# Activation pairs fetched one pair ahead, four products per x tile, and a last tile in two halves, in a one-core encoder layer

## The chip, the cores and the metric

The kernel runs on one core of one Trainium2 chip. The metric is device time in microseconds, from the first to the last instruction of the program, with little around them; lower is better. TensorE's clock has two levels here, 2.4 GHz (granted clock 1.00) and 1.2 GHz (0.50).

## The reference

One layer of an encoder on 512 tokens of 2048 channels, in fp32. Two branches start from the same normalised input, Hyena (long convolutions) and grouped-query attention; gates merge them, one projection follows, then a feed-forward block:

```python
h = rms_norm(x, mix_norm_g)
proj = h @ w_in                      # x0, x1, hv (Hyena), q, k, v, gates
u_h = centred_short_conv(u_h, hy_conv_w, hy_conv_b)
x0, x1, hv = jnp.split(u_h, 3, axis=-1)
filt = implicit_filter(S, flt_w1, ..., flt_freq)
z = hv * x1
y_h = (bidir_fft_conv(z, filt) + hy_bias * z) * x0
q, k = axial_rope(rms_norm(q, ...)), axial_rope(rms_norm(k, ...))
y_a = block_gqa_attention(q, k, v)
g_h, g_a = jnp.split(sigmoid(g + b_gate), 2, axis=-1)
x = x + (g_h * (y_h @ w_br_hyena) + g_a * (y_a @ w_br_attn)) @ w_out
h2 = rms_norm(x, ffn_norm_g)
out = x + (silu(h2 @ w_ffn_gate) * (h2 @ w_ffn_up)) @ w_ffn_down
```

D_FF is 5632, that is 44 tiles of 128 channels; the 2048 channels are 16 tiles (KT), the 512 tokens one free dimension (S).

## The kernel before, in words

Every fp32 product is made of three matmuls (mm3, lines 175 to 178): high part by high part, high by low, low by high. So each weight tile and each activation is split: ACT casts it to the high part, and DVE subtracts that from the raw tile.

**Plain products.** wblk (lines 156 to 173) hands out 128x128 weight blocks. Eight of them are one tile of 128x1024, loaded on SP's queue (line 168), cast by ACT (line 169, wh), subtracted by DVE (line 170, wl). There are two raw buffers (wr) and three of each part. Only the first two tiles come in pieces of XW blocks. group runs the 16 k steps of one 128x512 output, 48 matmuls.

**Side work.** step() is called behind every mm3 and runs the next step of generators that were queued: the filter network (mlp_gen, filter_gen), the long convolutions (conv_gen), the attention heads. Constants such as Q_WAIT count in such steps where a generator starts. flush() runs what is left. So the order on each engine is that of the program text, and a generator's work is laid between the main products.

**Start.** For each k an x tile is loaded and split, then XW = 2 products (x1 and hv of channel tile 0) take it. Behind the loop come 16 squares and adds for the token sums, then groups px01 and phv1 of channel tile 1; in the middle of phv1 (RS_STEP) token_rstd forms the sums (rs1ss), the reciprocal root, and its broadcast over the partitions (rs1bcp, then the copy rbc). short_conv needs rbc: it is 4 instructions, 3 of them on DVE, for each of x1, hv, x0. filter_gen makes fd, bd, then hs, hd on DVE, which TensorE transposes (ktp).

**Seven-product stages.** Gates (g), feed-forward (f) and the two halves of the down projection (d, e) run a scheme with seven products in place of eight on halves of the tokens and of the channels. x_sums makes the seven sums V of a pair of activation tiles (ACT and DVE), x_split their two parts X (one ACT cast, line 809, and one DVE subtract, line 810). run then takes four raw weight tiles per group (a11, a21, a22, a12; line 822 on SP's queue) from 8 raw buffers: two that wblk uses, tag rb in pool wq, and one more. It starts with X of the first pair.

**Down projection.** Each half has a plain part first: 16 output tiles m, each a group over 6 activations. The result dp is multiplied into dt (line 1186) and added into the DRAM tile x2d by a DMA on POOL's queue (add_up). At every even m the activations of pair m // 2 are loaded from DRAM (act_raw, ACT's queue, line 1125), summed and split. tmp, with five buffers, holds act_raw and dt. Then run does 8 groups with the eight X.

**Between.** The output projection takes merged tiles ms: m_load (ACT's queue) and m_split for m = 3 to 15 stand ahead of its first weight tile. The Hyena and attention branch groups b come behind flush().

**End.** The last two output tiles are finished by out_finish: a multiply (line 1161), an add (line 1168), a DMA.

Of the kernel before, what the change touches and what calls it, by code (L numbers as in the profile page):

```python
# [16 lines left out]
P = 128  # L17
# [12 lines left out]
GATES_AHEAD = 3  # L30
MLP_WAIT = 22
Z_WAIT0 = 16
N_WARM = 10
XW = 2
RS_STEP = 8
K_WAIT = 20
Q_WAIT = (25, 21)
# [20 lines left out]
def weight_blocks():  # L58

    def cols(name, c0, nk, k0=0, w=P):  # L60
        return [(name, (k0 + k) * P, c0, w) for k in range(nk)]

    def gates(m):
        return cols("w_in", C_GH + m * P, KT) + cols("w_in", C_GA + m * P, KT)

    out = []
    for q in range(NQ):
        for c in (2 * q, 2 * q + 1):
            x1, hv = cols("w_in", C_X1 + c * P, KT), cols("w_in", C_HV + c * P, KT)
            out += [b for pair in zip(x1, hv) for b in pair] if c == 0 else x1 + hv  # L70
        for c in (2 * q, 2 * q + 1):
            out += cols("w_in", C_X0 + c * P, KT)
    for c0, m in ((C_KV, None), (C_Q, 0), (C_Q + 512, 1), (None, 2)):
        out += cols("w_in", c0, KT, w=512) if c0 is not None else []
        out += gates(m) if m is not None else []
    for m in range(KT):
        out += cols("w_br_hyena", m * P, HT) + cols("w_br_attn", m * P, HT)

    def quarters(name, c0, c1, k0=0):
        for half, c in ((0, c0), (0, c1), (1, c1), (1, c0)):  # L80
            out.extend((name, (k0 + k) * P, c, P) for k in range(half, KT, 2))

    for m in range(GATES_AHEAD, KT):
        quarters("w_in", C_GH + m * P, C_GA + m * P)
    for k in range(KT):
        out += [("w_out", k * P, m * P, P) for m in range(WIDE)]
    for m in range(WIDE, KT):
        out += cols("w_out", m * P, KT)
    for j in range(0, FT, 2):
        for name in ("w_ffn_gate", "w_ffn_up"):  # L90
            quarters(name, j * P, (j + 1) * P)
    for f0 in (0, NSTD + KT):
        for m in range(KT):
            out += cols("w_ffn_down", m * P, NSTD, k0=f0)
        for m in range(0, KT, 2):
            quarters("w_ffn_down", m * P, (m + 1) * P, f0 + NSTD)
    return out


def layer_kernel(tc, wpk, xT, par, flt, zemb, w4, decT, tbl, tb2, rope, qkg, out):  # L100
# [55 lines left out]
    def wblk(nb=1):  # L156
# [8 lines left out]
        i, n = st["tile"] - 1, XW if st["tile"] <= 2 else BLK  # L165
# [79 lines left out]
    def sumsq_add(acc, src, k, name):  # L245
        if k == 0:
            nc.scalar.activation(acc, src, AF.Square)
        else:
            sq = tmp(f"{name}{k}")
            nc.scalar.activation(sq, src, AF.Square)  # L250
            nc.vector.tensor_tensor(acc, acc, sq, ALU.add)
# [238 lines left out]
    xg, xrs = [], []  # L490
    queue(mlp_gen())
    queue(filter_gen(0))
    for k in range(KT):
# [7 lines left out]
        xrs.append(xr)  # L501
# [4 lines left out]
    acc1 = tmp("acc1")  # L506
    for k in range(KT):
        sumsq_add(acc1, xrs[k], k, "xsq")
# [35 lines left out]
    for q in range(NQ):  # L544
        zl, zf_l = [], []
        for c in range(2):
            ct = 2 * q + c
            if ct < 2:
                p1, p2 = (xps, p2nd)[ct]
            else:  # L550
                p1 = ps_tile(f"px1{ct}")
                group(p1, xg)
# [16 lines left out]
        for c in range(2):  # L569
            ct = 2 * q + c  # L570
            p0 = ps_tile(f"px0{ct}")
            group(p0, xg)
            x0st[ct] = short_conv(p0, ct, f"x0{ct}", r3.tile([P, S], F32, tag="r", bufs=16, name=f"yh{ct}"))
# [203 lines left out]
    def seven(nm, gi, nv=3):  # L777
# [82 lines left out]
        def run(groups, c_tiles, finish, rows=None, sums=None, side_pool=None, norm=None, tail=None, each=None):  # L860
# [17 lines left out]
            for n in range(groups):  # L878
# [81 lines left out]

    flush()
    ats.release()
    at.release()
    yhs = [split(r1, t, "hi", "lo", 16, 16, f"yhs{i}") for i, t in enumerate(yh)]
# [17 lines left out]
    for m in range(KT):  # L982
        gs = []
        for i, src in enumerate((yhs, yas)):
# [3 lines left out]
            bp = ps_tile(f"b{i}{m}")  # L988
            group(bp, src)
# [61 lines left out]
    for m in range(3, KT):  # L1051
        m_load(m)
        m_split(m, r1, "ms", KT - 3)
# [105 lines left out]
    def out_finish(n, i, t):  # L1159
        m = 2 * n + i  # L1160
        nc.vector.tensor_tensor(t, t, rbc2, ALU.mult)
        if n < NP - 1:
            add_up(m, t)
            if n > 0:
                nc.gpsimd.dma_start(out[m - 2], x2d[m - 2])
            return
        nc.gpsimd.dma_start(out[m - 2], x2d[m - 2])
        nc.vector.tensor_tensor(t, t, lasts[i], ALU.add)
        nc.sync.dma_start(out[m], t)
# [9 lines left out]
    for half, f0 in enumerate((0, NSTD + KT)):  # L1179
        vp = tc.alloc_tile_pool(name=f"vpd{half}", bufs=1, reuse_waits="tile")  # L1180
        x_sums, x_split, V, run = seven("de"[half], None, 2)
        for m in range(KT):
            dp = ps_tile(f"d{half}{m}")
            group(dp, [acts[j] for j in range(f0, f0 + NSTD)])
            t = tmp(f"dt{half}{m}")
            nc.vector.tensor_tensor(t, dp, rbc2, ALU.mult)
            add_up(m, t)
            if m % 2 == 0:
                j = f0 + NSTD + m
                V[m // 2] = x_sums(m // 2, act_raw(j), act_raw(j + 1))  # L1190
                x_split(m // 2, V[m // 2], (0, 7))
# [3 lines left out]
        else:  # L1195
            run(NP, c_down, out_finish, each=last_rows)
# [115 lines left out]
```

## Time and profile before

| what | us |
|---|---|
| median of three runs | 2606.41 (2604.97 to 2608.80) |
| the profiled execution | 2606.41 |
| its span | 2604.6 |
| TensorE (PE) busy in it | 2550.0, 98% |
| DVE busy | 2017.0, 77% |
| ACT busy | 1205.6, 46% |
| POOL busy | 176.4, 7% |
| mean DMA rate | 133 GB/s |

A share over the whole span says little here: the program is a row of stages, and TensorE stands still at a few of their borders only. The views to read are therefore the list of TensorE's waits, and windows around them. In a window, PEclk is the mean granted clock, DMA the busy share of the 16 DMA engines. PEld is TensorE's weight loading, which runs beside the matmuls.

### The profile page before, as it was taken

The page shows a single profiled execution, that of the slowest core. Times are in us where ns is not written, and L with a number is a line of the kernel's source. Part 1 is how long each engine was busy: PE and PEld are TensorE (multiplying, and loading weights), DVE is VectorE, ACT ScalarE, POOL GpSimd, SP SyncE. Part 2 cuts the span into 40 slices and gives each one's busy share as a digit, 9 for nine tenths or more (in the row PEclk, how much of TensorE's full clock was granted, in tenths as well). Part 3 has the DMA queues.
Part 4 walks back from the last instruction along what each step waited for, and adds up shares of the span by engine and source line. Part 5 has one row for each costly group of instructions (what it writes and reads, how often), then busy time and mean ns, then how long its engine had stood idle before and what let it go on. Part 6 is the DMA issues. An engine that isn't in the chain of part 4 may idle for free.

```text
span 2604.6 us, 35152 instructions
## 1 busy us (share of the span) xinstructions
PE 2550.0 (98%) x13426; PEld 2186.7 (84%) x13426; DVE 2017.0 (77%) x2902; ACT 1205.6 (46%) x1796; POOL 176.4 (7%) x290
## 2 busy tenths in 40 slices
PE   9999999999999999999999999999999998999899
PEld 6788888878887888888788888888888887888688
DVE  7877763657555999754799889889889878887787
ACT  6444433647343445443444444444444445444443
POOL 1000001110000000000000000000000001001111
PEclk9999999999999999999999999999999999999899
DMA  6323233222454444544223333333333357447554
GB/s 223 110 95 116 94 116 107 73 77 91 169 185 138 158 148 143 183 156 144 101 105 130 115 120 130 115 121 130 114 121 130 114 159 205 138 126 195 155 156 105
DMA packets 112821, 345.74 MB, mean 133 GB/s; under 512 B 13835, under 2 KB 15371, under 8 KB 112428
## 3 DMA queue, kind: packets, MB, share of 16 engines
q1 hardware_dynamic: 70272, 248.02, 27.2%
q0 software_dynamic: 22112, 58.73, 8.7%
q10 hardware_dynamic: 20268, 36.74, 4.6%
q8 instruction: 105, 1.72, 0.3%
q14 instruction: 64, 0.52, 0.1%
HBM read 295.21 MB, written 51.90 MB: 133 GB/s over the span
## 4 chain that ended last, share of the span: by engine, by line
PE 63%; issue 27%; DVE 4%; DMA 2%; POOL 2%; ACT 2%; SPq 0%; POOLq 0%; ACTq 0%; DVEq 0%
PE fx L118 8%; PE b L118 7%; PE px L118 7%; PE o L118 6%; PE gx L118 5%; PE fy L118 4%; PE ex L118 3%; PE q L118 3%; PE phv L118 3%; PE gy L118 3%; PE fz L118 2%; PE ey L118 2%; PE kv L118 2%; POOL x2d L1145 1%; PE g L118 1%
## 5 line engine op out<-in xcount | busy, mean ns | idle before, releaser
L170 DVE TENSOR_TENSOR wl<-wr,wh 128x1024 fp32r<-128x1024 f32 (+1 forms) x178 | 211.7, 1189 | 180.3 <-ACT wh L169 179.2
L169 ACT CAST wh<-wr 128x1024 fp32r<-128x1024 f32 (+1 forms) x178 | 182.2, 1024 | 344.5 <-PE o L118 70.3
L841 ACT CAST fwhs<-fs 128x1024 fp32r<-128x1024 f32 x176 | 184.9, 1051 | 247.7 <-PE fx L118 115.6
L841 ACT CAST fwha<-fa 128x1024 fp32r<-128x1024 f32 x132 | 138.8, 1052 | 205.8 <-PE fx L118 102.4
L842 DVE TENSOR_TENSOR fwls<-fs,fwhs 128x1024 fp32r<-128x1024 f32 x176 | 214.6, 1220 | 10.6 <-ACT fwhs L841 3.8
L118 PE MATMUL fx<-fX,fwha 128*128 128x512 f32 x704 | 178.6, 395 | 3.7 <-DVE c L937 2.1
L118 PE MATMUL fx<-fX,fwhs 128*128 128x512 f32 x704 | 177.8, 395 | 1.9 <-DVE fv L857 1.9
L118 PE MATMUL fy<-fX,fwhs 128*128 128x512 f32 x704 | 176.9, 392 | 0.0
L842 DVE TENSOR_TENSOR fwla<-fa,fwha 128x1024 fp32r<-128x1024 f32 x132 | 161.1, 1221 | 5.1 <-ACT fwha L841 1.3
L118 PE MATMUL o<-ms,wh 128*128 128x512 f32 x512 | 159.0, 392 | 1.8 <-ACT wh L169 1.8
L118 PEld LDWEIGHTS fx<-fX,fwha 128*128 128x128 f32 x704 | 127.5, 190 | 27.5 <-DVE c L937 2.3
L118 PEld LDWEIGHTS fx<-fX,fwhs 128*128 128x128 f32 x704 | 127.7, 190 | 25.2 <-DVE fv L857 2.2
L118 PEld LDWEIGHTS fy<-fX,fwhs 128*128 128x128 f32 x704 | 126.6, 189 | 22.6
L118 PE MATMUL d<-act,wh 128*128 128x512 f32 x384 | 118.1, 389 | 0.0
L118 PEld LDWEIGHTS o<-ms,wh 128*128 128x128 f32 x512 | 96.8, 189 | 22.4 <-ACT wh L169 2.2
L118 PE MATMUL px<-xh,wh 128*128 128x512 f32 x272 | 109.2, 401 | 1.4 <-ACT wh L169 1.3
L118 PE MATMUL px<-xh,wl 128*128 128x512 f32 x272 | 107.5, 395 | 3.0 <-DVE wl L170 3.0
L835 DVE TENSOR_TENSOR fs<-fa,fa 128x1024 f32<-128x1024 f32 x88 | 106.9, 1215 | 0.3 <-DMA fa<-wpk 0.2
L118 PE MATMUL px<-xl,wh 128*128 128x512 f32 x272 | 107.1, 394 | 0.0
L835 DVE TENSOR_TENSOR fs<-fs,fa 128x1024 f32<-128x1024 f32 x88 | 107.0, 1215 | 0.1
L118 PEld LDWEIGHTS fx<-fX,fwla 128*128 128x128 f32 x704 | 96.5, 191 | 7.0
L118 PEld LDWEIGHTS fy<-fX,fwls 128*128 128x128 f32 x704 | 96.2, 190 | 6.9
(1224 smaller groups left out, 6247.8 us busy)
## 6 DMA issues: line engine op xcount, KB each, us to landing
fa<-wpk SPq DMA_DIRECT2D x176, 512.0 KB, 3.5
wr<-wpk SPq DMA_DIRECT2D x170, 512.0 KB, 3.5
ga<-wpk SPq DMA_DIRECT2D x52, 512.0 KB, 3.5
da<-wpk SPq DMA_DIRECT2D x32, 512.0 KB, 3.6
ea<-wpk SPq DMA_DIRECT2D x32, 512.0 KB, 3.6
actd<-c POOLq DMA_DIRECT2D x40, 256.0 KB, 4.9
actr<-actd ACTq DMA_DIRECT2D x40, 256.0 KB, 4.5
x2d<-dt POOLq DMA_DIRECT2D x32, 256.0 KB, 5.2
```

The source lines that it names most:

```text
L118: tc.keep_in_program_order(nc.tensor.matmul(out, lhsT=lhsT, rhs=rhs, start=start, stop=stop, **kw))
L169: nc.scalar.copy(st["hi"][:, c], st["raw"][:, c])
L170: nc.vector.tensor_tensor(st["lo"][:, c], st["raw"][:, c], st["hi"][:, c].bitcast(F32), ALU.subtract)
L835: nc.vector.tensor_tensor(t, a, b, ALU.add)
L841: nc.scalar.copy(hi, w)
L842: nc.vector.tensor_tensor(lo, w, hi.bitcast(F32), ALU.subtract)
L1145: nc.gpsimd.dma_start(x2d[m], t, accum_op=ALU.add)
```

## The change

Six parts, in the program's order.

1. XW becomes 4: the x loop feeds four products (x1 and hv of channel tiles 0 and 1), with the weights packed in that order. The first weight tile comes in pieces of two blocks, the second of four. The squares go into the loop. The group that token_rstd interrupts is now px00 (x0 of channel tile 0).
2. Q_WAIT of the second attention group is 26 steps instead of 21.
3. The first two Hyena branch groups (HYENA_FIRST) and the split of their inputs stand ahead of flush().
4. m_load and m_split for m = 3 to 15 move into the k loop of the output projection, five ahead.
5. Down halves: act_raw is issued one pair ahead, dt goes into raw buffers (tag rb, two outputs in one), the last pair's X is split in two cuts.
6. The last output tile is finished in two halves of 256 columns.

```diff
-XW = 2
+XW = 4
-Q_WAIT = (25, 21)
+Q_WAIT = (25, 26)
...
-        i, n = st["tile"] - 1, XW if st["tile"] <= 2 else BLK
+        i, n = st["tile"] - 1, {1: XW // 2, 2: XW}.get(st["tile"], BLK)
...
         for i in range(XW):
             wh, wl = wblk()
             mm3(xps[i], wh, wl, hi, lo, k == 0, k == KT - 1)
             step()
-    acc1 = tmp("acc1")
-    for k in range(KT):
-        sumsq_add(acc1, xrs[k], k, "xsq")
+        sumsq_add(acc1, xr, k, "xsq", work)
...
-    p2nd = [ps_tile("px01"), ps_tile("phv1")]
-    group(p2nd[0], xg)
-    group(p2nd[1], xg, 0, RS_STEP)
+    px00 = ps_tile("px00")
+    group(px00, xg, 0, RS_STEP)
     gen = token_rstd(acc1, "rs1", rs1)
     next(gen)
-    group(p2nd[1], xg, RS_STEP, KT)
+    group(px00, xg, RS_STEP, KT)
...
+    yhs = [split(r1, t, "hi", "lo", 16, 16, f"yhs{i}") for i, t in enumerate(yh)]
+    bps = [ps_tile(f"b0{m}") for m in range(HYENA_FIRST)]
+    for bp in bps:
+        group(bp, yhs)
     flush()
...
-    for m in range(3, KT):
-        m_load(m)
-        m_split(m, r1, "ms", KT - 3)
...
     for k in range(KT):
+        for m in range(max(3, len(ms)), min(k + 5, KT)):
+            m_load(m)
+            m_split(m, r1, "ms", KT - 3)
         for op in ops:
...
+        pairs = [[act_raw(f0 + NSTD + i) for i in (0, 1)]]
         for m in range(KT):
             dp = ps_tile(f"d{half}{m}")
             group(dp, [acts[j] for j in range(f0, f0 + NSTD)])
-            t = tmp(f"dt{half}{m}")
+            if m % 2 == 0:
+                t2 = wq.tile([P, 2 * S], F32, tag="rb", bufs=NRAW - 3, name=f"dt{half}{m}")
+            t = t2[:, m % 2 * S:(m % 2 + 1) * S]
             nc.vector.tensor_tensor(t, dp, rbc2, ALU.mult)
             add_up(m, t)
             if m % 2 == 0:
-                j = f0 + NSTD + m
-                V[m // 2] = x_sums(m // 2, act_raw(j), act_raw(j + 1))
-                x_split(m // 2, V[m // 2], (0, 7))
+                p = m // 2
+                if p + 1 < NP:
+                    pairs.append([act_raw(f0 + NSTD + m + i) for i in (2, 3)])
+                V[p] = x_sums(p, *pairs[p])
+                x_split(p, V[p], (0, 7) if p + 1 < NP else (0, 3, 7))
...
                 finish(n, 0, c0)
+                if halves and n == groups - 1:
+                    finish(n, 1, c1, slice(H, S))
                 d = ev(f"d_{n}")
                 nc.scalar.activation(d, x[:, :H], AF.Copy, scale=-1.0)
                 nc.vector.tensor_tensor(c1[:, :H], d, x[:, H:], ALU.subtract)
-                finish(n, 1, c1)
+                if halves and n == groups - 1:
+                    finish(n, 1, c1, slice(0, H))
+                else:
+                    finish(n, 1, c1)
```

The order of the instructions moves with it at many places. Three of them follow. A row is a line, an operation, what it writes and reads; the number behind a name tells tiles apart.

The output projection on ACT (ms is the high part of a merged tile, wh that of a weight tile, mg a merged tile as loaded). Before, up to its fourth weight tile (three casts of wh stand earlier):

```order
L1031 CAST ms_9854<-mg_9852 128x512
L1027 DMA mg_9862<-md_5898 128x512
L1027 DMA mg_9867<-md_5899 128x512
L1031 CAST ms_9859<-mg_9857 128x512
L1027 DMA mg_9872<-md_5900 128x512
L1031 CAST ms_9864<-mg_9862 128x512
L1031 CAST ms_9869<-mg_9867 128x512
L169 CAST wh_9975<-wr_9974 128x1024
L1031 CAST ms_9874<-mg_9872 128x512
L169 CAST wh_10005<-wr_10004 128x1024
```

Now:

```order
L1044 CAST ms_9860<-mg_9858 128x512
L1044 CAST ms_9883<-mg_9881 128x512
L1040 DMA mg_9898<-md_5824 128x512
L1040 DMA mg_9921<-md_5825 128x512
L1040 DMA mg_9938<-md_5826 128x512
L172 CAST wh_9944<-wr_9943 128x1024
L1044 CAST ms_9900<-mg_9898 128x512
L1044 CAST ms_9923<-mg_9921 128x512
L1044 CAST ms_9940<-mg_9938 128x512
L1040 DMA mg_9961<-md_5827 128x512
L1040 DMA mg_9978<-md_5828 128x512
L172 CAST wh_9984<-wr_9983 128x1024
```

The weight casts now stand between the casts of ms: before, twelve of the thirteen came ahead of the fourth wh.

SP's queue at the plain part of d (wr is a plain weight tile, da a raw tile of the seven-product stage, its number the group). Before, three raw tiles were issued ahead of the weights, the rest behind them:

```order
L822 DMA da_0_19778<-wpk 128x1024
L822 DMA da_0_19780<-wpk 128x1024
L822 DMA da_1_19957<-wpk 128x1024
L168 DMA wr_19208<-wpk 128x1024
...
L168 DMA wr_19713<-wpk 128x1024
L822 DMA da_0_19774<-wpk 128x1024
L822 DMA da_0_19776<-wpk 128x1024
L822 DMA da_1_19961<-wpk 128x1024
```

Now:

```order
L171 DMA wr_19671<-wpk 128x1024
L171 DMA wr_19704<-wpk 128x1024
L824 DMA da_0_19762<-wpk 128x1024
L824 DMA da_1_19947<-wpk 128x1024
L824 DMA da_0_19764<-wpk 128x1024
L824 DMA da_0_19766<-wpk 128x1024
L824 DMA da_0_19768<-wpk 128x1024
L824 DMA da_1_19945<-wpk 128x1024
```

All raw tiles stand behind the plain weights now. da_0_19766 (a22), da_0_19768 (a12) and da_1_19945 (a11 of group 1) go into buffers that held dt tiles, of m = 10 and 11, 12 and 13, 14 and 15.

ACT at the end of that plain part (actr is an activation as loaded, dV its sums, dX the cast of them). Before:

```order
L809 CAST dX_19602<-dV_19592 128x7x256
L1125 DMA actr_19655<-actd_5935 128x512
L1125 DMA actr_19657<-actd_5936 128x512
L841 CAST dwha_0_19785<-da_0_19774 128x1024
L793 ACTIVATE dV_19659<-actr_19655 128x256
L794 ACTIVATE db_19660<-actr_19655 128x256
L796 ACTIVATE dV_19659<-actr_19657 128x256
L797 ACTIVATE dV_19659<-actr_19657 128x256
L841 CAST dwhs_0_19810<-ds_0_19808 128x1024
L809 CAST dX_19669<-dV_19659 128x7x256
```

Now:

```order
L811 CAST dX_19595<-dV_19585 128x7x256
L811 CAST dX_19661<-dV_19651 128x7x256
L795 ACTIVATE dV_19719<-actr_19647 128x256
L798 ACTIVATE dV_19719<-actr_19649 128x256
L799 ACTIVATE dV_19719<-actr_19649 128x256
L172 CAST wh_19672<-wr_19671 128x1024
L1138 DMA actr_20875<-actd_5873 128x512
L1138 DMA actr_21074<-actd_5874 128x512
L811 CAST dX_19729<-dV_19719 128x3x256
L811 CAST dX_19729<-dV_19719 128x4x256
L172 CAST wh_19705<-wr_19704 128x1024
L843 CAST dwha_0_19773<-da_0_19762 128x1024
```

Before, the loads of a pair stood right ahead of its sums, and the casts of group 0 stood among the last pairs. Now the last pair's two casts of dX come ahead of the last plain weight tile and of group 0.

## Rows read from the trace of the kernel before

**Rows 1.** The page's first lines: span, then busy time, share and instructions.
```profile
span 2604.6 us, 35152 instructions
...
PE 2550.0 (98%) x13426; PEld 2186.7 (84%) x13426; DVE 2017.0 (77%) x2902; ACT 1205.6 (46%) x1796; POOL 176.4 (7%) x290
```

**Rows 2.** TensorE's waits: who waited for whom: us in total, times, longest.
```profile
PE ex L118 <- DVE eX L810: 13.0, 2, 10.6
PE dx L118 <- DVE dX L810: 8.6, 1, 8.6
PE qT10p L121 <- DVE q1o L646: 3.2, 2, 1.7
PE px L118 <- DVE wl L170: 3.0, 2, 2.5
PE rs1ss L118 <- issue: 2.2, 1, 2.2
...
PE o L118 <- ACT wh L169: 1.8, 1, 1.8
...
PE av L118 <- DVE pt170sl L191: 1.0, 1, 1.0
```

**Rows 3.** Windows: length, busy us (instructions) of PE, PEld, DVE, ACT, POOL; clock, DMA, GB/s.
```profile
5.60:50.00 44.40, 42.52 (x173) 31.23 (x173) 33.50 (x50) 31.24 (x52) 6.54 (x12) 1.00 0.85 278
50.00:90.00 40.00, 35.33 (x145) 27.67 (x144) 33.28 (x66) 16.03 (x23) 0.00 (x0) 0.91 0.24 81
62.50:95.62 33.12, 30.61 (x125) 23.89 (x124) 29.29 (x56) 13.97 (x22) 0.00 (x0) 0.95 0.26 86
570.00:585.00 15.00, 11.76 (x51) 9.23 (x50) 12.26 (x21) 6.89 (x11) 6.84 (x12) 0.89 0.25 87
1090.00:1105.00 15.00, 12.66 (x47) 9.63 (x47) 8.27 (x11) 7.27 (x10) 0.00 (x0) 0.89 0.54 175
2130.00:2195.00 65.00, 65.00 (x289) 53.77 (x287) 49.80 (x65) 32.92 (x49) 13.56 (x16) 1.00 0.84 213
2204.20:2207.60 3.40, 3.10 (x11) 2.87 (x12) 3.15 (x6) 2.66 (x4) 0.00 (x0) 0.50 1.01 360
2441.20:2446.50 5.30, 4.91 (x16) 4.24 (x17) 2.63 (x4) 1.42 (x2) 0.00 (x0) 0.50 0.32 128
```

**Rows 4.** Groups of ACT, 2100 to 2204: busy us, mean ns; idle before, its releasers.
```profile
L809 ACT CAST dX<-dV 128x1792 fp32r<-128x1792 f32 x8 | 13.6, 1696 | 12.6 <-DVE dV L800 12.6
...
L793 ACT ACTIVATE dV<-actr 128x256 f32<-128x256 f32 x8 | 3.3, 418 | 10.1 <-DMA actr<-actd 10.1
```

**Rows 5.** DMA issues, 2100 to 2204: count, KB each, median us to landing.
```profile
actr<-actd ACTq DMA_DIRECT2D x20, 256.0 KB, 4.5
x2d<-dt POOLq DMA_DIRECT2D x16, 256.0 KB, 5.1
da<-wpk SPq DMA_DIRECT2D x7, 512.0 KB, 5.3
```

**Rows 6.** Tile q1o: duration min/median/max in ns, first and last start.
```profile
L121 PE MATMUL qT10p<-ident,q1o x4: 270/300/328, 574.1 to 578.1; 128*128 128x128 f32 x4
```

**Rows 7.** Timeline of ACT, 640 to 643: start us, duration us.
```profile
640.90 1.28 ACT L750 ACT_TABLE_LOAD   x1
642.19 0.72 ACT L750 ACTIVATE gt<-gt,prm 128x512 f32<-128x512 f32 x1
```

**Rows 8.** Timeline of ACT at the output projection.
```profile
1095.24 1.04 ACT L169 CAST wh<-wr 128x1024 fp32r<-128x1024 f32 x1
```

**Rows 9.** Groups of DVE, 2100 to 2204, columns as in rows 4.
```profile
L810 DVE TENSOR_TENSOR dX<-dV,dX 128x1792 fp32r<-128x1792 f32 x8 | 16.2, 2022 | 4.9 <-ACT dX L809 4.8
L170 DVE TENSOR_TENSOR wl<-wr,wh 128x1024 fp32r<-128x1024 f32 x12 | 14.7, 1223 | 4.4 <-ACT wh L169 4.2
L1186 DVE TENSOR_TENSOR dt<-d,rbc 128x512 f32<-128x512 f32 x16 | 11.0, 687 | 4.8 <-PE d L118 4.8
...
L798 DVE SCALAR_TENSOR_TENSOR dV<-dV,db 128x256 f32<-128x256 f32 x8 | 3.4, 420 | 1.6 <-ACT dV L797 1.6
```

More of the change, by code (lines that the diff above doesn't have):

```diff
@@ L30 @@
 GATES_AHEAD = 3
+HYENA_FIRST = 2
 MLP_WAIT = 22
@@ L67, in weight_blocks @@
     for q in range(NQ):
-        for c in (2 * q, 2 * q + 1):
-            x1, hv = cols("w_in", C_X1 + c * P, KT), cols("w_in", C_HV + c * P, KT)
-            out += [b for pair in zip(x1, hv) for b in pair] if c == 0 else x1 + hv
+        pr = [cols("w_in", c0 + c * P, KT) for c in (2 * q, 2 * q + 1) for c0 in (C_X1, C_HV)]
+        out += [b for col in (pr if q else zip(*pr)) for b in col]
         for c in (2 * q, 2 * q + 1):
@@ L75, in weight_blocks @@
         out += gates(m) if m is not None else []
+    for m in range(HYENA_FIRST):
+        out += cols("w_br_hyena", m * P, HT)
     for m in range(KT):
-        out += cols("w_br_hyena", m * P, HT) + cols("w_br_attn", m * P, HT)
+        out += cols("w_br_hyena", m * P, HT) if m >= HYENA_FIRST else []
+        out += cols("w_br_attn", m * P, HT)
     def quarters(name, c0, c1, k0=0):
@@ L243, in token_rstd, with sumsq_add @@
         res["r"] = r
-    def sumsq_add(acc, src, k, name):
+    def sumsq_add(acc, src, k, name, new=tmp):
         if k == 0:
@@ L248, in sumsq_add @@
         else:
-            sq = tmp(f"{name}{k}")
+            sq = new(f"{name}{k}")
             nc.scalar.activation(sq, src, AF.Square)
@@ L489, in layer_kernel @@
     xps = [ps_tile(f"px{i}") for i in range(XW)]
-    xg, xrs = [], []
+    xg, acc1 = [], work("acc1")
     queue(mlp_gen())
@@ L548, in layer_kernel @@
             if ct < 2:
[L549 removed]
+                p1, p2 = xps[2 * ct:2 * ct + 2]
             else:
@@ L570, in layer_kernel @@
             ct = 2 * q + c
-            p0 = ps_tile(f"px0{ct}")
-            group(p0, xg)
+            if ct == 0:
+                p0 = px00
+            else:
+                p0 = ps_tile(f"px0{ct}")
+                group(p0, xg)
             x0st[ct] = short_conv(p0, ct, f"x0{ct}", r3.tile([P, S], F32, tag="r", bufs=16, name=f"yh{ct}"))
@@ L858, in fold, with run @@
             return t
-        def run(groups, c_tiles, finish, rows=None, sums=None, side_pool=None, norm=None, tail=None, each=None):
+        def run(groups, c_tiles, finish, rows=None, sums=None, side_pool=None, norm=None, tail=None, each=None, halves=False):
             raws["base"] = state["tile"]
@@ L987, in layer_kernel @@
                 nc.scalar.dma_start(gs[i], gd[i][m])
-            bp = ps_tile(f"b{i}{m}")
-            group(bp, src)
+            if i == 0 and m < HYENA_FIRST:
+                bp = bps[m]
+            else:
+                bp = ps_tile(f"b{i}{m}")
+                group(bp, src)
             if m < GATES_AHEAD:
@@ L1157, in early_acts, with out_finish @@
             act_split(j, act_raw(j), ea, "act", EARLY_ACTS)
-    def out_finish(n, i, t):
+    def out_finish(n, i, t, cols=slice(0, S)):
         m = 2 * n + i
-        nc.vector.tensor_tensor(t, t, rbc2, ALU.mult)
+        t = t[:, cols]
+        nc.vector.tensor_tensor(t, t, rbc2[:, cols], ALU.mult)
         if n < NP - 1:
             add_up(m, t)
[L1164 to L1169, printed above, removed]
+        else:
+            nc.vector.tensor_tensor(t, t, lasts[i][:, cols], ALU.add)
+            nc.sync.dma_start(out[m, :, cols], t)
+        if n > 0 and cols.stop == S:
+            nc.gpsimd.dma_start(out[m - 2], x2d[m - 2])
     lasts = []
@@ L1195, in layer_kernel @@
         else:
-            run(NP, c_down, out_finish, each=last_rows)
+            run(NP, c_down, out_finish, each=last_rows, halves=True)
     for p in (ea, xa, wq, pad, late["xb"], late["sg"], banks["pool"], tpool, wpool, dpool, cpool):
```

3 lines of the change are left out of this document (1 added, 2 removed).

## Prediction

> **What bounds the kernel now.** The page comes first. TensorE is busy for 2550.0 of the 2604.6 us span [rows 1], so work moved between the other engines pays only where TensorE stands still. The profiled execution took 2606.41 us, 1.8 more than its span, and that is also the median of the three runs (2604.97 to 2608.80); the sum below is made against 2606.4. A measurement of this kernel tells about 0.2% (5.2 us) from no change.
>
> The second view is TensorE's waits [rows 2]. They are few and each has a place: 13.0 and 8.6 us where the seven-product stage of each down half begins, for the last activation pair eX or dX; 3.2 in the second attention group's transposes; 2.2 before the token sums rs1ss; 2.5 (of 3.0) for a weight tile of the px products; 1.8 for the weight cast of the output projection; 1.0 before the last attention values, for pt170sl.
>
> The third view is windows [rows 3]. A wait costs twice. In the 3.4 us behind dX's wait the granted clock is 0.50, that is 1.2 instead of 2.4 GHz, and in 5.3 us behind eX's wait as well. Matmuls issued there take double time, so these two stretches gave away 1.7 and 2.65 us. Means of 0.91 over 50 to 90 us, 0.89 over 570 to 585 and 0.89 over 1090 to 1105 say 7.2, 3.3 and 3.3 us at the lower level, so up to 3.6, 1.65 and 1.65 us lost there. The plain part of d gives the pace without waits: 289 matmuls in 65.0 us, 0.225 each, at full clock.
>
> **The change, part by part.**
>
> *Down halves.* Why is X7 late? The plain part has 16 groups, 4.1 us each, two of them per activation pair, so a pair may take 8.2 us. ACT and DVE need less: DVE is busy for 49.8 of 65.0 us, ACT for 32.9 [rows 3]. But ACT's first sum waits 10.1 us in all for the load of actr, and its cast of X (1.70 us) waits 12.6 us in all for the sums [rows 4]. The load takes 4.5 us to landing [rows 5] and is issued only when a tile of the five tmp buffers is free; the products' results dt sit in the same five until their add into x2d has landed, 5.1 us after its issue. Load, sums, cast and subtract run one behind the other, and the last pair ends 8.6 us after TensorE wants it. The change issues each load a pair (8.2 us, more than 4.5) ahead and takes dt out of tmp. DVE's work in the plain part stays below 8.2 us per pair, so X7 should be ready about when the last group ends. Its two cuts add one instruction each to ACT and DVE, ahead of the last group's end. Gain: d 8.6 + 1.7 = 10.3; e 13.0 + 2.65 = 15.6.
>
> What is late next: dt now lies in the three two-part buffers that the first raw tiles of the seven-product stage also use. Three raw loads that were issued ahead of the plain part now stand behind its weights on SP's queue, and a22 of group 0 waits for the adds of m = 10 and 11, a12 for 12 and 13, and a11 of group 1 for 14 and 15. An add lands 5.1 us after its issue, and a load of da takes 5.3 in this stretch [rows 5]. With E the end of the plain part, the group of m = 11 ends at E - 16.4, its add lands by about E - 10.6, a22 by E - 5. The group of 13 ends at E - 8.2, its add lands at E - 2.4, a12 at E + 2.9. Group 0 begins with a11, whose buffer no dt holds. A product there is 8 matmuls of 512 and 8 of 256 columns, 2.7 us at the pace above: a21 + a22 is wanted for the second at E + 2.7, a12 for the fourth at E + 8.1, each some 3.5 us earlier for its sum, cast and subtract (1.2, 1.05 and 1.2 us), that is at E - 0.8 and E + 4.6. Margins of 4 and 1.7 us: I take no wait, and keep 0 to 5.3 plus 1.7 of clock per half for the range.
>
> *Start.* From 5.6 to 50.0 us 173 matmuls stand in 44.4 us; at 0.225 they need 38.9. About 5.5 us are ramp and waits while the DMA engines are 85% busy at 278 GB/s [rows 3]. A k step loads an x tile of 256 KB and two weight blocks of 64 KB for six matmuls (1.35 us): 291 GB/s, more than is delivered. With four products it is 512 KB per 2.7 us, 194 GB/s. I take 4.5 of the 5.5, since the first tiles still have to arrive (bounds 2 and 5.5). The squares now run inside the loop, so rs1ss finds its sum: 2.2, and half of this stretch's 3.6 of clock, 4.0 together.
>
> The wait of 2.5 for wl comes from DVE's row of short convolutions, behind which that weight subtract stood [rows 2]. It goes, but something takes its place. The reciprocal's broadcast rs1bcp now comes a whole group (48 matmuls, 10.8 us) and more later against the filter's steps: between it and the first ktp transposes stood 126 product matmuls, now 78, with the 8 fp in either. That is 78 x 0.225 + 8 x 0.23 = 19.4 us for TensorE. DVE's work from the first u to the last hd, which the transposes read, filled 29.3 us [rows 3]. Four of its five weight subtracts (1.2 each) and the filter network's rows (about 4.8) no longer lie in between: 19.7. Add 1.3 for the broadcast's way to DVE and an estimated 2 for the second decay tile, whose load is now issued late (between 0 and the 4.5 of an actr load): 23.0. So ktp waits 3.6 us, more than the 2.5 removed, and the clock falls again (1.8): 4.3 gained, 5.4 given back, -1.1. Bounds: +4.3 (all hidden) and -3.6.
>
> *Second attention group five steps later.* Its first four transposes run from 574.1 to 578.1 us [rows 6], 3.2 of it waiting for q1o, whose own work is not moved. Five steps are 15 matmuls more ahead of them, 3.4 us: the last would be wanted at 577.8 instead of 574.4 and comes at 578.1. 0.3 is left, and the clock's 1.65 goes too: 4.55.
>
> *Hyena products ahead of the attention tail.* Three matmuls (0.7 us) now stand between the last transposes and the values, where 1.0 us was waited, but the sigmoid of the gates moves ahead of pt160sh on ACT. The rows give 1.28 us for its table load and 0.72 for itself, back to back [rows 7], so pt160 comes about 2 us later. I take 0, between -1.5 and +1. The Trainium skill (ScalarE: Activation LUTs, "What ACT_TABLE_LOAD costs") counts a drain as well, about 2.7 us a switch; by that figure the tail would lose about 1.4 us and the sum would be 40.5. Here the sigmoid starts 1.29 us after the load does, so the trace shows no such drain behind it.
>
> *Output projection.* Twelve of the thirteen casts of m = 3 to 15 stood ahead of the fourth weight tile's cast, the one from 1095.24 [rows 8]; now it stands among them, and each ms is asked for five k steps later than it is issued. Wait 1.8, clock 1.65: 3.45. Bounds 1.5 and 4.
>
> *Last tile in halves.* A DVE step on 512 columns takes 0.69 us, one on 256 takes 0.42 [rows 9]. Two steps stand behind the last product: 0.54, and a little of the last transfer: 0.6 (bounds 0.2 and 1.3). The copy of the tile before, on POOL's queue, is issued behind the first half's steps and lands beside the second half's.
>
> **Sum:** 10.3 + 15.6 + 4.5 + 4.0 - 1.1 + 4.55 + 0 + 3.45 + 0.6 = 41.9, so 2606.4 - 41.9 = 2564.5.
>
> **Rivals.**
> *A, a new wait at the seven-product stages.* The adds or the raw loads land late, as above. For it: the DMA engines are already 84% busy in the plain part, 101% just behind it [rows 3]. The Trainium skill (DMA: Bandwidth & Descriptors, "Issuing engines are not separate DMA queues") says that transfers of all issuing engines share the same 16 DMA engines; by that rule, moving 1.5 MB of raw loads into the busiest stretch delays everything there, the adds too. By the rows, 1.5 MB at the 360 GB/s of [rows 3] are 4.4 us, the price of one such wait, with 1.7 of clock 6.1; both halves 12.2: 2577. Against: a11 is not held, and the margins above.
> *B, X7 still late.* The chain is bound by DVE instead of the loads, since DVE's rows for a pair (subtract 2.02, two dt of 0.69, sums of 0.42, one and a half wl of 1.22) make 6.9 of 8.2 us [rows 9] and any wait eats into it. If half of 25.9 stays: 2577.
> *C, the start gives little.* The ktp wait grows by its 2.5 to the bound and the ramp gives 2: 2569.5. Nothing in the rows speaks for both at once.
> *D, slower than before.* dt tiles come free only when their adds have landed. If adds, which now share three double buffers, run one behind another on POOL's queue at over 4.1 us each, DVE's dt waits, the product's bank with it, and TensorE stops in every group: 32 groups times the excess. It decides when one add takes over 5.4 us alone (32 x 1.35 = 43); at 6 us it takes back 60.8, and the time would be 2625. Against: before, 16 adds kept up with 4.1 us each though 5.1 to landing, so they overlap.
> *E, nothing moves.* The order shows the loads and casts moved, so this is nearly excluded.
>
> **Numbers.** Forecast 0.62, A 0.17, B 0.12, C 0.05, D 0.02, E 0.02. Range 2554 to 2580: at the low end the start reaches its upper bounds (1 and 5.4 us more), the tail, the projection and the end theirs (1, 0.5 and 0.7): 2556, and two for terms that I hold smaller than they are; at the top A or B with 3 us less from the start. Faster 0.96, same 0.02, slower 0.02.
>
> **What would show it.** In the changed profile: no wait for dX or eX over 1 us, and the granted clock at 1.00 behind both (right); a wait on a22, a12 or their sums there (A); X's subtract ending behind the last group of the plain part (B); a ktp wait of 3 to 4 us near 70 us and no rs1ss wait (start); qT10p waits under 0.5; no output-projection wait. Wrong if the waits of [rows 2] at d and e come back under other names, or if matmuls in the plain parts lose the 0.225 pace (D).

## The result, and the profile after

The changed kernel takes 2574.78 us (median of four runs, 2572.69 to 2580.39) against 2605.76: a ratio of 0.9882, interval 0.9865 to 0.9900. That is 31 us faster, inside the range and on the forecast side, but 10.3 us short of the sum. Its profiled execution took 2574.66 us, with a span of 2572.9.

The page's first lines answer to [rows 1]:

```profile
span 2572.9 us, 35107 instructions
...
PE 2542.2 (99%) x13426; PEld 2183.0 (85%) x13426; DVE 2012.9 (78%) x2904; ACT 1200.7 (47%) x1794; POOL 176.5 (7%) x290
```

TensorE's waits answer to [rows 2]; the columns are total, times and longest:

```profile
PE av L121 <- ACT pt170sh L193: 2.3, 1, 2.3
PE av L121 <- ACT pt160sh L193: 2.2, 1, 2.2
...
PE px L121 <- ACT wh L172: 1.6, 1, 1.6
...
PE ex L121 <- DVE dc L939: 1.5, 2, 1.2
PE ktp L124 <- DVE hd L363: 1.4, 1, 1.4
...
PE dx L121 <- DVE dv L859: 1.1, 1, 1.1
PE dx L121 <- DVE dc L939: 1.0, 1, 1.0
```

The two large waits for dX and eX are gone, and so are those for q1o, rs1ss and the output projection's wh. At the head of the list now stand two waits of the attention's tail, which the sum had at nothing.

To see what each stage is worth, clock and waits together, take the distance from each matmul's start to the next and subtract the pace of its width (0.227 us for 512 columns, 0.120 for 256, 0.109 for 128, as they run one behind the other at full clock). What is left is time lost. Summed by stage, from one execution of each kernel (the first 4 us, where TensorE only warms up, are left out here and below):

| stage (us of the span) | lost before | lost after | gain | the sum's term |
|---|---|---|---|---|
| start (4 to 100) | 16.2 | 12.4 | 3.8 | 7.4 |
| second attention group (550 to 600) | 5.6 | 0.5 | 5.1 | 4.55 |
| attention's tail (600 to 650) | 3.8 | 7.8 | -4.0 | 0 |
| gates' first group (800 to 850) | 6.6 | 6.3 | 0.3 | none |
| output projection (1050 to 1150) | 4.6 | 0.1 | 4.5 | 3.45 |
| d (2100 to 2300) | 11.8 | 3.8 | 8.0 | 10.3 |
| e (2350 to 2450) | 15.8 | 3.1 | 12.7 | 15.6 |
| behind the last matmul's start | 6.0 | 4.7 | 1.3 | 0.6 |

The gains add up to 31.7, the difference of the spans. So the missing 10 us lie in four places: start 3.6, tail 4.0, d 2.3, e 2.9, with about 2.5 found elsewhere. A row is good to 1 or 2 us only; how far a stage differs between kernels that are alike there stands at the head of the experiments.

**The tail.** ACT's timeline of the changed kernel (start, duration, idle before and its releaser):

```profile
628.95 1.28 ACT L752 ACT_TABLE_LOAD   x1
630.24 0.72 ACT L752 ACTIVATE gt<-gt,prm 128x512 f32<-128x512 f32 x1
...
631.34 0.59 ACT L193 CAST pt160sh<-pt 128x512 fp32r<-128x512 f32 x1
...
633.10 6.46 ACTq L997 DMA_DIRECT2D gr<-gd  x2
639.60 0.58 ACT L193 CAST pt170sh<-pt 128x512 fp32r<-128x512 f32 x1 [6.67 <-DMA gd<-gt]
```

The cast pt160sh is 2 us late for the table load and sigmoid, as foreseen. But pt170sh stands behind something else: the issue of two gr loads takes 6.46 us, because one of them needs the tmp buffer that the last gates gt leave only when their store gd has landed. The cast behind them starts only when they are issued, after 6.67 us in which ACT does nothing, and TensorE waits for it.

**The start.** A window from 3 to 30 us of the changed kernel (length, busy PE, PEld, DVE, ACT, POOL, clock, DMA share, GB/s), then when POOL issued the first and the last table load T, then how long an x tile took to land (count, KB each, median us):

```profile
3.00:30.00 27.00, 26.04 (x113) 19.86 (x111) 20.70 (x33) 20.05 (x34) 4.41 (x8) 1.00 1.04 358
```

```profile
6.62 0.70 POOL L513 DMA_DIRECT2D T<-tbl  x1 [5.30 <-ACT acc L250]
...
20.45 0.53 POOL L513 DMA_DIRECT2D T<-tbl  x1 [0.74 <-issue]
```

```profile
xr<-xT SPq DMA_DIRECT2D x16, 256.0 KB, 6.9
```

The DMA engines are full, though the sum said 194 GB/s would do. Before, POOL issued T from 35.8 us on, in the same order of the program. T reuses the buffers of the x tiles; with the squares inside the loop these come free one after another, and so 2.1 MB that nobody needs yet move into the loop.

**d and e.** The three buffers that dt uses are half of the stage's raw buffers: those are six (two that wblk uses, three of tag rb, one more), not the eight named at the start. DVE's timeline at the first group of d:

```profile
2189.25 1.23 DVE L837 TENSOR_TENSOR ds<-ds,da 128x1024 f32<-128x1024 f32 x1 [1.58 <-DMA da<-wpk]
2190.39 0.42 DVE L859 TENSOR_TENSOR dv<-dx,dv 128x256 f32<-128x256 f32 x1
```

The sum s4 waits 1.58 us for its raw tile, and the fold dv, which frees the bank that TensorE wants next, stands behind it on DVE. That is rival A in small. The clock did not fall for it in this execution (windows from about the end of the plain part, columns as above):

```profile
2181.00:2196.00 15.00, 13.90 (x75) 11.83 (x74) 12.22 (x15) 7.66 (x12) 1.73 (x2) 1.00 0.63 154
2405.00:2420.00 15.00, 14.89 (x79) 12.64 (x78) 10.58 (x12) 4.09 (x7) 1.73 (x2) 1.00 0.71 179
```

Elsewhere it did. The wait for dc, behind e's second group, is 1.2 us here with the clock at 1.00. In three of the kernels below whose part 5 is the change's (gate loads on POOL, squares later, tables held) it is 1.8 to 2.3 us, and the granted clock of 2450 to 2454 us is 0.57 to 0.62. With the tables held (the wait, then the window):

```profile
PE ex L121 <- DVE dc L940: 2.5, 2, 2.3
```

```profile
2450.00:2454.00 4.00, 3.65 (x11) 3.02 (x12) 4.00 (x6) 0.36 (x1) 0.00 (x0) 0.62 0.00 0
```

With the start undone the same happens at d, behind a wait for dv of 2.4 us (granted clock 0.72 from 2196 to 2202 us). So rival A's clock term, too, comes in some executions.

### The profile page after: what moved, and what is told of

Its sections match the earlier page's. It is cut to its first block, busy times and chain, and to the rows that moved or that the text cites. A ratio compares the mean times of both kernels' runs of the same rounds, so it can differ in the third digit from the quotient of the medians.

```text
span 2572.9 us, 35107 instructions
## 1 busy us (share of the span) xinstructions
PE 2542.2 (99%) x13426; PEld 2183.0 (85%) x13426; DVE 2012.9 (78%) x2904; ACT 1200.7 (47%) x1794; POOL 176.5 (7%) x290
## 4 chain that ended last, share of the span: by engine, by line
PE 61%; issue 29%; DVE 5%; POOL 2%; ACT 2%; DMA 1%; SPq 0%; POOLq 0%; ACTq 0%; DVEq 0%
PE fx L121 8%; PE o L121 7%; PE b L121 7%; PE px L121 6%; PE gx L121 5%; PE fy L121 4%; PE q L121 3%; PE ex L121 3%; PE gy L121 3%; PE phv L121 3%; PE fz L121 2%; PE kv L121 2%; PE ey L121 2%; POOL x2d L1158 1%; PE gz L121 1%
## 5 line engine op out<-in xcount | busy, mean ns | idle before, releaser
L844 DVE TENSOR_TENSOR fwls<-fs,fwhs 128x1024 fp32r<-128x1024 f32 x176 | 214.7, 1221 | 10.3 <-ACT fwhs L843 2.5
L121 PE MATMUL px<-xh,wh 128*128 128x512 f32 x288 | 115.7, 402 | 1.6 <-ACT wh L172 1.6
L121 PE MATMUL px<-xh,wl 128*128 128x512 f32 x288 | 114.1, 396 | 0.5 <-DVE wl L173 0.5
L121 PE MATMUL px<-xl,wh 128*128 128x512 f32 x288 | 113.5, 394 | 0.0
L121 PEld LDWEIGHTS fx<-fX,fwls 128*128 128x128 f32 x704 | 96.9, 192 | 7.0
```

The costliest lines, as they stand in the source:

```text
L121: tc.keep_in_program_order(nc.tensor.matmul(out, lhsT=lhsT, rhs=rhs, start=start, stop=stop, **kw))
L844: nc.vector.tensor_tensor(lo, w, hi.bitcast(F32), ALU.subtract)
```

## The experiments

All are edits of the changed kernel but for one of the kernel before. The four or more runs of one kernel lie 2 to 9 us apart, so small effects are looked for in the profiles: in a stage's loss and in its named waits. A stage's loss varies as well. Among the profiles whose stage is as in the change, it is 9.9 to 12.4 us at the start (six profiles; of that 6.3 to 8.4 up to 50 us), 6.9 to 8.8 in the tail (seven), 3.4 to 6.3 at d and 2.8 to 7.1 at e up to 2500 us (six each). The change's own profile is the highest of these at the start (12.4) and among the lower ones at d and e. A difference inside such a spread shows nothing by itself; a wait that no other profile has does.

**Gate loads on POOL's queue.**

```diff
-                nc.scalar.dma_start(gs[i], gd[i][m])
+                nc.gpsimd.dma_start(gs[i], gd[i][m])
```

> The six loads of stored gates (gr) are issued on POOL's queue instead of ACT's; all else as in the change. Theory: in the changed kernel the cast pt170sh stands on ACT behind the issue of a gr load, which needs the tmp buffer that the last gates leave only when their store has landed; ACT stands still for 6.7 us, and TensorE waits 2.3 + 0.3 us for it, with a stretch at the lower clock. Then the wait for pt170sh falls under 0.5 us, the wait for pt160sh (2.2 us, table load and sigmoid ahead of it) stays, and the region from 600 to 650 us loses 3 us of its 7.8 over the plain pace: about 2572. Rival: the table load is the whole of the tail's loss; then both waits stay and the time stays at 2574.7.

Measured: 2574.26 us, ratio to before 0.9888 (0.9869 to 0.9907). The tail lost 5.7 us instead of 7.8, and the wait for pt170sh is gone from TensorE's list; ACT no longer stands still for a store. The wait for pt160sh grew:

```profile
PE av L121 <- ACT pt160sh L193: 3.0, 1, 3.0
```

In the order that the compiler made of this kernel the sigmoid lies between two exponentials, and there is a second table load ahead of pt160sh (ACT's timeline):

```profile
626.72 1.28 ACT L752 ACT_TABLE_LOAD   x1
628.01 0.73 ACT L752 ACTIVATE gt<-gt,prm 128x512 f32<-128x512 f32 x1
...
629.36 1.28 ACT L690 ACT_TABLE_LOAD   x1
630.65 0.69 ACT L690 ACTIVATE p<-sp,sm 128x512 f32<-128x512 f32 x1
```

So pt170sh's wait was the gr load, as the theory said, but 2.1 us came back instead of 3, and the whole time can't be told from the change's. What is left of the tail's loss goes with the wait for pt160sh, behind the table load and the sigmoid. In all three places shown, the next function starts 1.29 us after the load does, where the Trainium skill (ScalarE: Activation LUTs, "What ACT_TABLE_LOAD costs") has 2.66 us with a drain; the measurement decides.

**Results in tmp again.**

```diff
-            if m % 2 == 0:
-                t2 = wq.tile([P, 2 * S], F32, tag="rb", bufs=NRAW - 3, name=f"dt{half}{m}")
-            t = t2[:, m % 2 * S:(m % 2 + 1) * S]
+            t = tmp(f"dt{half}{m}")
```

> Only the place of the plain part's results is undone: dt lies in the five tmp buffers again; the activation pairs are still asked for one pair ahead. Theory: the five buffers were the limit, and dt held them until its add had landed; then the loads cannot run ahead although they are asked for earlier, and the waits for dX and eX come back nearly whole (7 to 9 and 10 to 13 us): 2592 to 2601. Rival: asking one pair ahead is enough, and only the raw tiles' wait of 1.1 us goes away: 2573 to 2576.

Measured: 2579.14 us, 0.9906 (0.9885 to 0.9926). Both numbers missed: it lies between, nearer to the rival. d lost 7.1 and e 4.6 us (6.9 up to 2500 us), against 3.8 and 3.1 (3.4) in the change and 11.8 and 15.8 before; only d's lies outside the spread.

```profile
PE dx L121 <- DVE dX L812: 1.5, 1, 1.5
...
PE dx L121 <- ACT dwha L843: 1.4, 1, 1.4
```

Of the 8.6 us for dX 1.5 are back, a wait that no profile with dt in the raw buffers has, and ACT is late for the first weight cast. Asking a pair ahead does most of the work even with shared buffers.

**Pairs not asked for ahead.**

```diff
-                if p + 1 < NP:
-                    pairs.append([act_raw(f0 + NSTD + m + i) for i in (2, 3)])
+                if p:
+                    pairs.append([act_raw(f0 + NSTD + m + i) for i in (0, 1)])
```

> The other half of that part is undone: dt stays in the raw buffers, but each pair's loads are asked for at the pair itself. Theory (buffers were the limit): the compiler's order puts the loads ahead by itself once a buffer is free, so X7 is in time as in the change: 2573 to 2577, no wait for dX or eX over 1 us. Rival (asking early is what counts): half or more of the two waits comes back, 8 us or more: over 2582.

Measured: 2575.30 us, 0.9892 (0.9873 to 0.9910), with no wait for dX or eX. As the theory had it: with dt out of tmp the loads run ahead whether they are asked for early or not; at d the last pair's split ends at 2169.5 us, 11.6 us before the first product that could use it. With the run above: either half of the edit breaks the chain; the whole wait needs both of the old halves.

**Squares later.**

```diff
-        sumsq_add(acc1, xr, k, "xsq", work)
+        if k >= 5:
+            sumsq_add(acc1, xrs[k - 5], k - 5, "xsq", work)
+    for k in range(KT - 5, KT):
+        sumsq_add(acc1, xrs[k], k, "xsq", work)
```

> In the x loop the square of a tile is taken five tiles later than its split. Theory: the wait of 1.6 us for the weight cast at 28.7 us is ACT's order: four splits and four squares of x tiles that TensorE wants later stood ahead of that cast, which ran 2.3 us after its tile had landed. With fewer squares in front the cast comes about 1 to 1.5 us earlier, that wait falls to 0.5 or less, and the clock does not fall behind it: 2 to 3 us less in the first 50 us. Rival: the weight tile is late because x tiles take the DMA engines and a raw buffer comes free late; then the wait stays over 1 us.

Measured: 2576.71 us, 0.9893 (0.9874 to 0.9912). The theory is not borne out: the wait came earlier (1.2 us for wh at 23.6 us, 0.5 for wl behind it), and the first 50 us lost 8.5 us instead of 7.2. But the run does not decide between theory and rival: in the other five profiles with the change's start the wait for that wh is 0 to 0.9 us without any edit. This led to the DMA engines and to the table loads.

**Tables held.** A copy of one column makes each T tile wait for the last x tile's split; the load then overwrites it.

```diff
+            nc.scalar.copy(t[:, :1], xg[KT - 1][0][:, :1].bitcast(F32))
             nc.gpsimd.dma_start(t, tbl[i, j])
```

> The eight DCT table loads (T, 256 KB each, POOL's queue) wait for the split of the last x tile, as the four CS loads already do; all else as in the change. Theory: with the squares in the x loop, x buffers come free there, and the T loads that reuse them moved from 36 to 42 us into 6.6 to 20.5 us, 2.1 MB in a stretch where the DMA engines are full; x and weight tiles come late for it, and this took back the gain of the ramp. Then xr lands in about 5 us instead of 6.9, the wait for wh (0 to 1.6 us at 29 us) goes, and the first 50 us lose 4 to 5 us over the plain pace instead of 7 to 8: 2 to 3 us less in all. Rival (ACT's order of squares alone): the waits of the first 50 us stay as they are.

Measured: 2574.86 us, 0.9885 (0.9870 to 0.9900), runs from 2570.9 to 2578.5: no difference that the time can show. In the profile the mechanism is there (the same window, and the landing of x tiles):

```profile
3.00:30.00 27.00, 27.00 (x116) 21.85 (x115) 22.28 (x36) 22.07 (x38) 0.00 (x0) 1.00 0.84 284
```

```profile
xr<-xT SPq DMA_DIRECT2D x16, 256.0 KB, 5.8
```

TensorE is busy for all of the 27 us, x tiles land in 5.8 us instead of 6.9, and no wh is waited for up to 60 us. The landing repeats: 6.4 to 7.0 us in the seven profiles where the table loads run in the loop of four products, 5.3 to 5.8 in the three where they are held. So the table loads do crowd the x tiles. What it costs TensorE is less than the theory had: the first 50 us lost 6.0 us, and 5.0 and 6.0 in the two later kernels with held tables, against 6.3 to 8.4 without; on average some 1.5 us, of a ramp that was to give 4.5. Up to 100 us the loss of 10.6 lies inside the spread. The wait of 1.3 us for the filter network's h at 38 us is no price of the edit: five of the six profiles with the change's start have it at 1.4. That the queues of SP and POOL share the engines agrees with the Trainium skill (DMA: Bandwidth & Descriptors, "Issuing engines are not separate DMA queues").

**Attention undone.**

```diff
-HYENA_FIRST = 2
-Q_WAIT = (25, 26)
+HYENA_FIRST = 0
+Q_WAIT = (25, 21)
```

> The second attention group starts after 21 steps again and no Hyena product stands ahead of the flush; the rest as in the change. Theory: the two edits gave 5.1 us at the transposes (waits for q1o and the clock) and took 2 to 4 us at the tail (pt160sh, pt170sh). Undone, the two q1o waits (1.5 and 1.7 us) are back, and the tail has its 2.2 us of waits as before: 1 to 3 us slower than the change, 2576 to 2578. Rival (the Hyena products cover the tail): the tail gets worse without them and the whole is 5 us or more slower, over 2580.

Measured: 2578.17 us, 0.9897 (0.9883 to 0.9912): 3.4 slower than the change by the medians, just above the theory's end; the two intervals overlap. The waits for q1o are back (3.3 us; that stage loses 7.1), and the tail loses 3.5 instead of 7.8, both far outside what other profiles vary. So by the profiles these two parts together are worth 2.3 us; the tail gave back most of what the transposes won.

**Last results in tmp.**

```diff
-            if m % 2 == 0:
+            if m < 14 and m % 2 == 0:
...
-            t = t2[:, m % 2 * S:(m % 2 + 1) * S]
+            t = t2[:, m % 2 * S:(m % 2 + 1) * S] if m < 14 else tmp(f"dt{half}{m}")
```

> Only the last two results of each plain part (m = 14 and 15) go to the tmp buffers, so that the three raw buffers come free one pair (8.2 us) earlier. Theory: what is left at d and e (waits for dv and dc, 1.1 + 1.0 and 1.2 us) comes from raw tiles that land late: a sum that waits for its raw tile holds up the folds behind it on DVE. With the raw tiles earlier those waits fall by half or more: d and e lose 2 to 3 us less, 2572. Rival (DVE simply has too much to do in the first groups): the waits stay within 0.5 us of what they were.

Measured: 2577.62 us, 0.9898 (0.9881 to 0.9914). At d the loss fell from 3.8 to 2.7 (one wait for dv of 1.7 us in place of 1.1 and 1.0), but e lost 7.2, with a new wait:

```profile
PE ex L121 <- DVE ev L859: 4.8, 1, 4.8
```

Neither theory had that. A cause shows on ACT: the loads xl of the last two output rows, which are needed only at the very end, are issued there at the start of e's first group and wait for the adds of m = 14 and 15 (ACT's timelines of this kernel and of the changed one):

```profile
2412.88 1.99 ACT L843 CAST ewhs<-es 128x1024 fp32r<-128x1024 f32 x2 [7.15 <-DMA x2d<-dt]
```

```profile
2410.82 2.00 ACT L843 CAST ewhs<-es 128x1024 fp32r<-128x1024 f32 x2 [11.78 <-DMA x2d<-dt]
```

In the change ACT stands still longer, but mostly under the plain part: the first xl load is issued at 2410.37 us, 1.5 us behind that part's end (2408.89). Here it is issued at 2412.44, 7.3 us behind the end (2405.13), since the adds came later; the weight sum's cast and subtract follow it, and the fold ev behind them. This is read from the timelines; results in tmp with xl held were not run together. Whether late raw tiles or too much work on DVE cause the remaining waits at d and e is not settled by this run.

**The kernel before, with the last rows held.** The xl loads stood there too, ahead of e's last cast of X (ACT's timeline of the kernel before):

```profile
2432.52 5.18 ACTq L1177 DMA_DIRECT2D xl<-x2d  x2
2437.79 1.69 ACT L809 CAST eX<-eV 128x1792 fp32r<-128x1792 f32 x1 [5.13 <-DMA x2d<-dt]
```

```diff
-    def last_rows(n):
-        if n == NP - 1:
-            for m in (KT - 2, KT - 1):
-                lasts.append(tmp(f"xl{m}"))
-                nc.scalar.dma_start(lasts[-1], x2d[m])
...
             add_up(m, t)
+            if m == KT - 4:
+                for j in (KT - 2, KT - 1):
+                    lasts.append(tmp(f"xl{j}"))
+                    nc.scalar.copy(lasts[-1][:, :1], t[:, :1])
+                    nc.scalar.dma_start(lasts[-1], x2d[j])
```

> The kernel before with one edit: the loads of the last two output rows (xl) on ACT wait for the result of the seventh group. Theory: in the kernel before they stood on ACT ahead of the last cast of eX and waited 5.1 us for the adds into the rows that they read; this is why e's wait (10.6 + 2.3) is longer than d's 8.6, and the change takes it away with the rest. Then e's waits fall to 8 to 10 us and the time to 2600 to 2603. Rival (e waits longer for another reason): both stay, 2605.5.

Measured: 2601.23 us (ten runs), 0.9986 (0.9976 to 0.9996).

```profile
PE ex L118 <- DVE eX L810: 10.3, 2, 8.7
PE dx L118 <- DVE dX L810: 9.7, 2, 8.6
```

e's longest wait is now as long as d's, 8.7 and 8.6 us, and e loses 12.8 instead of 15.8. So 2.7 us of e's 13.0 were the xl loads, and the rest the chain that d has too. The total wait is 0.3 above the expected end. That the time came out as expected is in part luck: it fell by 5.6 us against the kernel before in the same rounds (2606.80), and e accounts for 3.0; in the profile the start, which the edit does not touch, lost 3.0 less as well.

**Start undone.** Part 1 of the change is taken back: XW = 2, the weights' old order, squares behind the loop, px01 and phv1 ahead of the broadcast. The core of it:

```diff
-XW = 4
+XW = 2
...
-        sumsq_add(acc1, xr, k, "xsq", work)
+    acc1 = tmp("acc1")
+    for k in range(KT):
+        sumsq_add(acc1, xrs[k], k, "xsq")
...
-    px00 = ps_tile("px00")
-    group(px00, xg, 0, RS_STEP)
+    p2nd = [ps_tile("px01"), ps_tile("phv1")]
+    group(p2nd[0], xg)
+    group(p2nd[1], xg, 0, RS_STEP)
```

> Only the start is undone: two products meet each x tile, the 16 squares come behind the loop, px01 and phv1 ahead of the broadcast; the rest as in the change. By the account of the two profiles over the plain pace the start's share of the gain is 3.8 us (first 100 us: 16.2 lost before, 12.4 after), not the 7.4 of the sum: then 2578 to 2581. Rival (the sum's term holds, and the loss is elsewhere): 2582 or more. Rival (the start gives nothing): 2574 to 2576.

Measured: 2579.12 us, 0.9893 (0.9875 to 0.9911): 4.3 above the change by the medians, with overlapping intervals. rs1ss (2.7) and wl (2.5) are waited for again; no kernel with the new start waits for rs1ss, or over 0.5 us for wl. The start loses 15.9 us; the three profiles with the old start lose 13.2 to 16.2, the six with the new one 9.9 to 12.4, on average 3.5 less. Part of the 4.3 is d, which lost 6.3 here without an edit.

**All mended, twice.** First the table loads held, gate loads on POOL, the last results in tmp, and more Hyena products in the tail:

```diff
+TAIL_WAIT = 4
...
                 turn(u - 1)
-                yield T_WAIT
+                yield T_WAIT + (TAIL_WAIT if g and u >= 7 else 0)
```

> The change with four mends together: table loads held, gate loads on POOL's queue, the last two results in tmp, and four more steps of Hyena products between the last transposes of the attention and their values. By the theories of the single ones: 2 to 3 us from the start, 2 to 6 from the tail, 2 to 3 from d and e: 2563 to 2569. If only the start is real: 2572.

Measured: 2573.99 us, 0.9880 (0.9865 to 0.9895). The tail lost 1.6 us instead of 7.8, the start 8.7 instead of 12.4, but e 8.1 instead of 3.1: the wait for ev (4.9) came with the last results in tmp, as in the run with that edit alone, and ate part of the gain. So that edit was left out, and the xl loads were held as above:

> The change with four mends: table loads held until the last x tile is split, gate loads on POOL's queue, four more steps of Hyena products between the last transposes and values of the attention, and the xl loads held until the seventh group of e. The last results stay in the raw buffers. From the profiles: 2 from the start, 4 to 6 from the tail (as with the four mends before), 1 to 2 at e, where ACT stood still for 11.8 and 2.7 us behind the xl loads: 2564 to 2568. If the waits of e's first groups come from late raw tiles alone, no gain at e: 2568 to 2570.

Measured: 2566.60 us (2566.24 to 2568.40), ratio to before 0.9852 (0.9837 to 0.9866), the fastest of all kernels here and 8 us below the change; its slowest run lies 4 us below the change's fastest.

```profile
PE dx L122 <- DVE dv L861: 1.6, 2, 1.2
PE ex L122 <- DVE dc L941: 1.5, 1, 1.5
PE ktp L125 <- DVE hd L364: 1.4, 1, 1.4
...
PE av L122 <- DVE pt160sl L195: 0.7, 1, 0.7
```

The tail loses 1.7 (change 7.8) and e 2.2 (3.1); start 12.1 (12.4), d 3.5 (3.8). What is shown to be won is the tail. The gate loads alone gave 2.1 us there; the four more steps were not run by themselves. e's 0.9 is less than what e varies by itself, and nothing can be shown at the start up to 100 us: with the tables held the wait for wh at 29 us is gone, but at 50 us 1.3 us are waited for one.

## Why the prediction was right, and where it was short

- *Down halves, 25.9 us.* Right in mechanism: no wait for dX or eX is left, and the clock stays at 1.00 behind both. That buffers held by dt and late loads made one chain is shown from both sides: with either half of the edit X7 is in time or nearly so. 20.7 came. The step that failed is "I take no wait" for the raw tiles: 1.0 to 1.2 us are waited at three places, for folds and results that the first two groups of d and e make on DVE. By DVE's timeline the margins were worked out for the product that needs a raw tile, but the sum that waits for it holds up the folds, and these free TensorE's banks. That is rival A's mechanism, small and without its clock term in this execution; that late raw tiles are the cause is read from the timeline, and the run that freed their buffers earlier did not settle it. That e's wait was longer than d's for the xl loads wasn't seen; it did not matter for the sum, since both went.
- *Start, 7.4 us.* 3.8 came, and 3.5 on the averages of the three profiles with the old start and the six with the change's. The term for rs1ss was right: the wait is gone. The ktp wait was foreseen as the successor and is there, but 1.8 us at 91 us instead of 3.6 near 70. The ramp's 4.5 is the term that failed: the first 50 us lost 7.2 us against 6.4 before, and 7.1 against 7.4 on the same averages. The rate of 194 GB/s counted SP's queue alone; POOL's, with the eight table loads that the freed x buffers let loose, was left out. Held back, they give some 1.5 of the 4.5; what took the rest stays open.
- *Attention's transposes, 4.55 us.* 5.1 came; no wait for q1o is left.
- *Tail, 0 us.* It lost 4.0, outside the bounds of -1.5 and +1. The 2 us for the table load and sigmoid were right, but against 0.7 us of products they already leave a loss, and the sum still took nothing. What failed above all is that the gr loads, five of which also moved ahead of pt170sh on ACT, were not followed: one waits for a buffer, and ACT waits with it for 6.7 us.
- *Output projection, 3.45 us.* 4.5 came: wl's wait of 0.5 went as well, which the bound of 4 had left out.
- *End, 0.6 us.* 1.3 came. The two shorter steps gave the 0.5 of the sum. From the last DVE step's end to the end of the span it is 2.6 us instead of 3.4, where the sum had almost nothing; four of the other kernels with this end have 3.0. Half the bytes in the last transfer are the likely reason, but that was not tried by itself.
- *The rivals.* C (start gives little, 2569.5) came true in the ramp, not at ktp; B, D and E did not happen. That the time still lies in the range is in part luck: its upper end was kept for A or B at full size, and the room was used by the tail, which no rival had, the ramp, and A in small.

## What to carry to other kernels

A load that is issued early waits early too: when an edit moves a DMA issue, or frees a buffer sooner, look up which queue it stands in, which buffer it writes and who held that last, and what compute instruction stands behind it in the same queue. Loads for the next stage (gr) kept ACT idle for 6.7 us, loads for the very end (xl) for 5.1 us in the kernel before, and loads of later tables (T) made x tiles land about 1 us later. Holding such a load with a one-column copy from the right producer kept xl and T back. When a rate is worked out for a loop, count the bytes of every queue that can run then, not only of the one that feeds it. And before a stage's loss is read from one profile, look how far the same stage differs between profiles of kernels that are alike there.

## What the runs showed that was not expected

The same waits can cost different amounts. At the first group of the feed-forward stage, which no edit touches, TensorE waits 2.1, 1.9 and 1.6 us in every one of the 13 profiles. The granted clock of the 40 us from its first matmul was not the same, in the changed kernel and in the fastest one:

```profile
1247.00:1287.00 40.00, 34.34 (x179) 29.50 (x178) 33.67 (x52) 24.11 (x33) 0.54 (x1) 0.91 0.24 86
```

```profile
1243.00:1283.00 40.00, 34.35 (x187) 29.36 (x186) 34.94 (x53) 24.25 (x33) 0.54 (x1) 0.96 0.25 86
```

A mean of 0.91 is 7.2 us at the lower level, 0.96 is 3.2. From 5 us ahead of that matmul to 50 us behind it 10.5 us are lost in the one and 9.0 in the other, with the waits the same. All 13 profiles fall into these two groups: five lose 10.4 to 10.6, eight 9.0. So a clock term of about 1.5 us can come or stay away with the same waits, and a part of the 2 to 9 us between runs of one kernel may be just this; that it is the whole of it wasn't tried.
